# Gated input with tokens on partitions turned by VectorE, queries and keys turned by VectorE, attention's loads at the ordinary rank

## The chip, the core and the metric

The kernel runs on one NeuronCore of a Trainium2 chip. Its engines work at the same time and wait for one another through semaphores: TensorE (PE, matmuls and transposes into the accumulator memory PSUM; its weight loads are listed as PEld), VectorE (DVE), ScalarE (ACT), GpSimd (POOL), and SyncE (SP), which here issues almost all DMAs. Each engine works through its own queue in order. The metric is the time of one execution on the device in microseconds (us); lower is better.

## The reference

One layer of a streaming encoder for 384 tokens: 256 of a prompt and 8 x 16 of running streams, 2048 features, all in float32. The part that the change touches, cut short:

```python
h = rmsnorm(x, norm_mix_g)
proj = h @ w_in        # columns: gated input 2 x 1024 | q 1024 | k 1024 | v 1024 | 8 forget logits | gates 2 x 2048
u = glu_in[..., :D_CONV] * jax.nn.sigmoid(glu_in[..., D_CONV:])
ext = jnp.concatenate([conv_buf, u], axis=1)
z = layernorm(causal_dwconv(ext, conv_dw_w, conv_dw_b), conv_ln_g, conv_ln_b)      # 31 taps
a_out = (z * jax.nn.sigmoid(z)) @ conv_pw_out
new_conv = ext[:, -(CONV_W - 1):]                                                  # an output
q = rmsnorm(q, q_norm_g); k = rmsnorm(k, k_norm_g)                                 # per head of 128; k, v are outputs
logf = jax.nn.log_sigmoid(f_logit + b_forget)
b_out = attn_fn(q, k, v, logf) @ w_att_out     # 8 heads; the 128 cached rows of each stream are read as well
x = x + (gate_a * a_out + gate_b * b_out) @ w_out
...                                            # second norm, up-projection, 3-tap conv, SiLU, down-projection
```

## The kernel before

**Matmuls in three products.** Every large matmul is done on split operands: a float32 is written as hi + lo, and hi x hi, hi x lo and lo x hi are added up in PSUM. A weight tile of 256 rows by up to 512 columns is fetched by SP into `raw` (three buffers, L133 to L139), ScalarE rounds it to `hi` (L145), VectorE makes `lo` as the difference (L146). `plan` lists these tiles in the order in which they are used; `ahead` fetches and splits two or three tiles in advance at a priority 150 places ahead (`SPLIT_AHEAD`), so that the planner which orders the instructions of each engine puts them early. Evacuations of PSUM have 400 (`EVAC_AHEAD`).

**Jobs.** `gemm` (L221) runs jobs one after another. A job of kind "B" has the tokens as stationary operand: for each of 16 k steps, three token blocks of 128 times three products, 512 columns of weights moving (9 matmuls a step). A job of kind "A" has the weights stationary: four blocks of 128 output columns, the 384 tokens moving (12 matmuls of 384 columns a step). The accumulators come from a pool `acc` of 5 PSUM banks and, for the third block of the second job of a pair, from `misc`, of 3 banks, which also serves every transpose and every attention step. After each k step of a job `tick` advances the generators in `sides` by one yield: their PE instructions are written into PE's order at that place. PE's order is the order of the program (`manual_schedule`, L291); the other engines are ordered by the planner. `queued` (L92) ties an instruction behind the last one so tied on its engine. `after(n, fn)` calls fn n ticks later.

**Stages, in PE's order**: 5 warm-up matmuls; the V columns as a pair of jobs with 344 columns each (V0 and V1), while `first_norm` transposes 16 chunks of x on PE (`x_chunk`, L282) and evacuates them as hi and lo of hT (L288, L289), then works out the row factors `rs1` and, by a matmul with a diagonal (L334), the same factors along the free dimension, `rs1b`; V2 alone, with the forget logits; K with `bias_rows` beside it (L483 on; small transposes and matmuls for the forget bias, written to DRAM and read back per head); Q; the gated input (four jobs of kind "A"), with attention and the depthwise conv as sides; the gates (eight jobs), with the rest of the conv and its layer norm; attention's and conv's projections in turns (`AO_PW`); w_out; the up and down projections.

**Attention**, one head every 6 ticks (L651 on): `head_past_keys` turns the cached keys on VectorE (L571) and loads the next head's; `head_operands` transposes the head's queries and keys on PE (L583, L587, three transposes each) and evacuates them (L584, L588); `head_scores` (L595 to L614), `head_probs`, `head_out` and `head_last` follow 4, 9, 11 and 13 ticks after the first. `load_v` fetches the cached values and the bias rows (`bs`) of a head together.

**The conv.** `conv` (L686 on) yields 24 + 7 x 17 + 31 times: channel block c starts at step 24 + 17c. Three ticks before its first tap `fill` builds the padded input `ext`; in it PE transposes the block's last rows (L708, L709), which ScalarE copies (L710, L711) and SP stores (L712, L713). The 31 taps of a block update `ut[:, c]` in place on VectorE (L720, L722); GpSimd adds the finished blocks into `sm` (L725, L727). After the conv's last yield, PE's matmul of `layer_norm` on `sm` (L779) stands in the gates stage. `blocks` (L255) turns token rows into feature rows on VectorE: 16 transposes by 32 x 32 blocks, each on 32 partitions (L259); the later stages use it for mixT, yT, extf and uT.

## Time and profile before

| what | value |
|---|---|
| median of 3 runs (lowest, highest) | 2005.14 us (2003.96, 2006.22) |
| profiled execution | 2005.83 us, span 2003.9 us |
| V columns, 344 wide (first matmul to K) | 7.21 to 85.74 us |
| K and Q | 85.74 to 218.46 us |
| gated input with attention | 218.46 to 390.05 us |
| gates with the rest of the conv | 390.05 to 655.17 us |
| attention's and conv's projections | 655.17 to 786.74 us |
| w_out | 786.74 to 919.73 us |
| up and down projections (last one from 1901.25) | 919.73 us to the end |

The stages are told by the first start of a large matmul of each in the timeline of PE.

How to read it: a row of the timeline is start, duration (both us), engine, line of the program, operation, tiles as out<-in, operands, count, and in brackets the engine's idle time before it with what ended it. A group's row ends in busy time, mean duration in ns, then idle time before and its releasers. Matmuls are pipelined: each lasts longer than the distance to the next one's start.

### The profile page before, as it was taken

Reading aid. Unit: us, or ns where it says so; the run is one execution under the profiler, and the core shown is the slowest. Engines: PE = TensorE matmul, PEld = TensorE weight load, DVE = VectorE, ACT = ScalarE, POOL = GpSimd, SP = SyncE. Lnnn points to the kernel's source line nnn. Section 1 sums busy time; section 2 is a strip of 40 time slices with the busy share of each in tenths; the row PEclk is TensorE's granted clock in tenths of the full one; section 3 lists DMA queues with packets and bytes.
Section 4 is the critical chain, followed back from the end, with each engine's and each line's share of the span. In section 5 each row is a group of like instructions: output and inputs, shape, how many; then the busy total and the mean of one; then the engine's idle time right before and its main releaser. Section 6 shows DMA issues by size and latency. Waiting matters only on the chain.

```text
span 2003.9 us, 24493 instructions
## 1 busy us (share of the span) xinstructions
PE 1992.6 (99%) x9431; PEld 1681.5 (84%) x9431; DVE 1272.2 (63%) x1852; ACT 742.1 (37%) x1077; POOL 87.2 (4%) x216
## 2 busy tenths in 40 slices
PE   8999999999999999999999999999999999999999
PEld 8988999988888887888888888888888888888887
DVE  4435478888765487676867683367673376638663
ACT  5434455433334523334433432233332233323321
POOL 2000001100000000000010000001000000000000
PEclk9999999999999999999999999999999999999999
DMA  6566566444444334534444444444443444344443
GB/s 179 176 175 175 137 163 167 120 140 131 132 134 125 127 121 142 185 121 133 127 137 116 137 127 137 126 127 126 129 135 127 133 120 137 126 129 125 137 157 106
DMA packets 209254, 275.99 MB, mean 138 GB/s; under 512 B 55878, under 2 KB 96729, under 8 KB 209129
## 3 DMA queue, kind: packets, MB, share of 16 engines
q1 hardware_dynamic: 208817, 273.85, 46.3%
q8 instruction: 74, 1.21, 0.2%
q0 software_dynamic: 288, 0.57, 0.2%
q14 instruction: 43, 0.35, 0.1%
q10 hardware_dynamic: 32, 0.01, 0.0%
HBM read 266.98 MB, written 7.86 MB: 137 GB/s over the span
## 4 chain that ended last, share of the span: by engine, by line
PE 95%; DVE 4%; issue 1%; DMA 1%; ACT 0%; SPq 0%; ACTq 0%; DVEq 0%
PE acc L244 28%; PE acc L246 28%; PE acc L245 28%; PE acc L239 2%; PE acc L241 2%; PE acc L240 2%; DVE mixT L259 1%; DVE lo L146 1%; DMA raw<-in_w_in_dram 1%; DVE sgA L843 0%; DVE uT L259 0%; DVE sgA L844 0%; PE misc L636 0%; PE misc L603 0%; PE misc L285 0%
## 5 line engine op out<-in xcount | busy, mean ns | idle before, releaser
L146 DVE TENSOR_TENSOR lo<-raw,hi 128x1024 fp32r<-128x1024 f32 (+2 forms) x481 | 579.6, 1205 | 582.7 <-ACT hi L145 579.0
L145 ACT CAST hi<-raw 128x1024 fp32r<-128x1024 f32 (+2 forms) x481 | 496.0, 1032 | 994.2 <-PE acc L246 869.1
L244 PE MATMUL acc<-hi,xg 128*128 128x512 f32 x1056 | 411.8, 390 | 0.0
L246 PE MATMUL acc<-hi,xg 128*128 128x512 f32 x1056 | 410.9, 389 | 0.0
L245 PE MATMUL acc<-lo,xg 128*128 128x512 f32 x1056 | 410.8, 389 | 0.0
L244 PE MATMUL acc<-hi,hT 128*128 128x512 f32 (+1 forms) x704 | 268.5, 381 | 2.4 <-ACT hT L288 2.4
L246 PE MATMUL acc<-hi,hT 128*128 128x512 f32 (+1 forms) x704 | 266.0, 378 | 0.4 <-DVE hT L289 0.4
L245 PE MATMUL acc<-lo,hT 128*128 128x512 f32 (+1 forms) x704 | 265.8, 377 | 0.0
L244 PEld LDWEIGHTS acc<-hi,xg 128*128 128x128 f32 x1056 | 198.2, 188 | 42.3
L246 PEld LDWEIGHTS acc<-hi,xg 128*128 128x128 f32 x1056 | 198.2, 188 | 41.3
L245 PEld LDWEIGHTS acc<-lo,xg 128*128 128x128 f32 x1056 | 198.2, 188 | 40.6
L244 PE MATMUL acc<-hi,act 128*128 128x512 f32 x528 | 205.5, 389 | 0.5 <-DVE y L1018 0.5
L246 PE MATMUL acc<-hi,act 128*128 128x512 f32 x528 | 205.4, 389 | 0.0
L245 PE MATMUL acc<-lo,act 128*128 128x512 f32 x528 | 205.4, 389 | 0.0
L722 DVE SCALAR_TENSOR_TENSOR ut<-ext,cw,ut 128x384 f32<-128x384 f32 x240 | 151.5, 631 | 6.1
L244 PEld LDWEIGHTS acc<-hi,hT 128*128 128x128 f32 x704 | 132.7, 189 | 25.3 <-ACT hT L288 2.7
L246 PEld LDWEIGHTS acc<-hi,hT 128*128 128x128 f32 x704 | 132.7, 189 | 23.3 <-DVE hT L289 0.7
L245 PEld LDWEIGHTS acc<-lo,hT 128*128 128x128 f32 x704 | 132.8, 189 | 22.2
L259 DVE STREAM_TRANSPOSE extf<-tok 32x384 f32<-32x384 f32 x176 | 100.3, 570 | 30.9 <-ACT tok L954 28.2
L259 DVE STREAM_TRANSPOSE uT<-tok 32x384 f32<-32x384 f32 x176 | 100.3, 570 | 29.7 <-ACT tok L954 26.9
L244 PEld LDWEIGHTS acc<-hi,act 128*128 128x128 f32 x528 | 99.1, 188 | 21.6 <-DVE y L1018 0.9
L245 PEld LDWEIGHTS acc<-lo,act 128*128 128x128 f32 x528 | 99.1, 188 | 20.5
(289 smaller groups left out, 2079.7 us busy)
## 6 DMA issues: line engine op xcount, KB each, us to landing
raw<-in_w_up_dram SPq DMA_DIRECT2D x176, 512.0 KB
raw<-in_w_in_dram SPq DMA_DIRECT2D x96, 512.0 KB
raw<-in_w_down_dram SPq DMA_DIRECT2D x88, 512.0 KB
raw<-in_w_in_dram SPq DMA_DIRECT2D x64, 256.0 KB
raw<-in_w_out_dram SPq DMA_DIRECT2D x32, 512.0 KB
raw<-in_w_att_out_dram SPq DMA_DIRECT2D x16, 512.0 KB
raw<-in_conv_pw_out_dram SPq DMA_DIRECT2D x16, 512.0 KB
raw<-in_w_in_dram SPq DMA_DIRECT2D x23, 344.0 KB
```

The source lines that it names most:

```text
L145: nc.scalar.copy(hi[:, k, :o], raw[:, k, :o])
L146: tt(lo[:, k, :o], raw[:, k, :o], f(hi[:, k, :o]), op=ALU.subtract)
L239: mm(o, hi[:, kk, s], ah, start=st, stop=False)
L240: mm(o, hi[:, kk, s], al, start=False, stop=False)
L241: mm(o, lo[:, kk, s], ah, start=False, stop=sp)
L244: mm(o, ah[:, s], hi[:, kk, :n], start=st, stop=False)
L245: mm(o, ah[:, s], lo[:, kk, :n], start=False, stop=False)
L246: mm(o, al[:, s], hi[:, kk, :n], start=False, stop=sp)
L259: nc.vector.transpose(put(a, slice(32 * b, 32 * b + 32)), src[32 * a:32 * a + 32, b])
L722: stt(o, v, wc, o, op0=ALU.mult, op1=ALU.add)
```

## The change

- **Gated input**: its four jobs have the tokens stationary, as all others. Its result `ur` has tokens on partitions, is multiplied by `rs1` as a per-partition factor, and `blocks` turns it into `ut`. `rs1b` and the matmuls that made it go. `ur` is also the conv state that is stored, by two DMAs after the fourth job; the transposes, copies and 16 DMAs in `fill` go.
- **Queries and keys**: the stages run V0 with V2, then Q, K, and V1 alone. After each, VectorE turns the normed rows by `blocks`: queries into `attT` (whose head's place is later overwritten by the head's output), keys into the memory of `qt`. The transposes on PE and their evacuations in `head_operands` go.
- **Order of attention**: `head_past_keys` becomes part of `head_operands` at tick 1; outputs and last step come at 12 and 14. The steps have a priority 250 places ahead; the loads of the cache and bias rows stay outside it, with values and bias loaded apart (`load_b`).
- **Conv**: CONV_FIRST 32 and CONV_LAG 15 in place of 24 and 17.
- **Accumulators**: `wide=True` puts the third block of every job into `misc`, in all stages but V, V1 and the gated input.
- **Start**: the identity, the splits of the first 20 tiles, the chunks' evacuations, the last squares, the root and the small loads on GpSimd are tied in program order with `queued`; the last squares and the norm come without yields after the last chunk.

```diff
-CONV_FIRST, CONV_LAG = 24, 17
+CONV_FIRST, CONV_LAG = 32, 15
-SPLIT_AHEAD, EVAC_AHEAD = 150, 400
+SPLIT_AHEAD, ATT_AHEAD, EVAC_AHEAD = 150, 250, 400
...
-        nc.scalar.activation(s, m, AF.Sqrt)
+        queued(nc.scalar.activation(s, m, AF.Sqrt), in_first())
...
-        nc.scalar.copy(hi[:, k, :o], raw[:, k, :o])
-        tt(lo[:, k, :o], raw[:, k, :o], f(hi[:, k, :o]), op=ALU.subtract)
+        first = in_first()
+        queued(nc.scalar.copy(hi[:, k, :o], raw[:, k, :o]), first)
+        queued(tt(lo[:, k, :o], raw[:, k, :o], f(hi[:, k, :o]), op=ALU.subtract), first)
...
-    planned(w_in, 0, V_COLS[0], 16, V_COLS[1])
-    for cols in V_COLS[2:] + K_COLS + Q_COLS + GLU_COLS + GA_COLS + GB_COLS:
+    planned(w_in, 0, V_COLS[0], 16, V_COLS[2])
+    for cols in Q_COLS + K_COLS + V_COLS[1:2] + GLU_COLS + GA_COLS + GB_COLS:
...
+    def in_first():
+        return len(plan) >= v_last - 4
...
-    def gemm(jobs, sides=()):
+    def gemm(jobs, sides=(), wide=False):
...
-                nb = 4 if j["kind"] == "A" else NTT
-                j["ps"] = [(misc_tile if j is not js[0] and i == 2 else acc_tile)() for i in range(nb)]
+                j["ps"] = [(misc_tile if i == 2 and (wide or j is not js[0]) else acc_tile)() for i in range(NTT)]
...
+                    if "post" in j:
+                        j["post"]()
...
-        nc.scalar.activation(hi, ps[:, :NT], AF.Identity, scale=g)
-        stt(lo, ps[:, :NT], g, f(hi), op0=ALU.mult, op1=ALU.subtract)
+        with tc.high_priority(offset=EVAC_AHEAD):
+            queued(nc.scalar.activation(hi, ps[:, :NT], AF.Identity, scale=g))
+            queued(stt(lo, ps[:, :NT], g, f(hi), op0=ALU.mult, op1=ALU.subtract))
...
-    gemm([job("B", 16, ha, tok_evac(kt, 512 * i, 512, 0)) for i in range(2)], [bias_rows()])
+    gemm([tok_job(qt, 512 * i, 512, 1) for i in range(2)], [norm_steps, bias_rows()], wide=True)
...
+    def q_panel(n):
+        blocks(qt[:, :, 512 * n:512 * (n + 1)], by_feature(attT[:, 4 * n:4 * n + 4]))
+        for h in range(4 * n, 4 * n + 4):
+            nc.scalar.activation(attT[:, h], attT[:, h], AF.Identity, scale=qgs[:])
+
+    kT = qt[:].rearrange("p t n -> p (t n)").rearrange("p (h x) -> p h x", h=H)
+
+    def k_panel(n):
+        blocks(kt[:, :, 512 * n:512 * (n + 1)], by_feature(kT[:, 4 * n:4 * n + 4]))
+
+    for n in range(2):
+        after(2 + 10 * n, lambda n=n: q_panel(n))
+    gemm([tok_job(kt, 512 * i, 512, 0) for i in range(2)], wide=True)
...
+    for n in range(2):
+        after(3 + 10 * n, lambda n=n: k_panel(n))
+    gemm([v_jobs[1]])
...
     def head_operands(d):
-        hs = d["hs"]
-        d["vc"], d["bs"] = vbs[d["h"]]
-        qT = p_att.tile([P, NT], F32, tag="qT", bufs=2, name="qT")
-        kT = p_att.tile([P, NT], F32, tag="kT", bufs=2, name="kT")
-        ps = misc_tile()
-        for t in range(NTT):
-            tr(ps[:, t * P:(t + 1) * P], qt[:, t, hs], ident[:])
-        nc.scalar.activation(qT[:], ps[:, :NT], AF.Identity, scale=qgs[:])
-        ps = misc_tile()
-        for t in range(NTT):
-            tr(ps[:, t * P:(t + 1) * P], kt[:, t, hs], ident[:])
-        nc.vector.tensor_copy(kT[:], ps[:, :NT])
-        nc.vector.tensor_copy(qz[d["h"] % 2][:, :, :, 0:16], by_stream(qT[:, 2 * P:]))
+        head_past_keys(d)
+        d["bs"] = bss[d["h"]]
+        nc.vector.tensor_copy(qz[d["h"] % 2][:, :, :, 0:16], by_stream(attT[:, d["h"], 2 * P:]))
...
-            for off, step in ((0, head_past_keys), (2, head_operands), (4, head_scores), (9, head_probs),
-                              (11, head_out), (13, head_last)):
+            for off, step in ((1, head_operands), (4, head_scores), (9, head_probs),
+                              (12, head_out), (14, head_last)):
...
-                step(d)
-                if step is head_out and d["h"] + 2 < H:
-                    load_v(d["h"] + 2)
+                with tc.high_priority(offset=ATT_AHEAD):
+                    step(d)
+                if step is head_operands and d["h"] + 1 < H:
+                    load_k(d["h"] + 1)
+                if step is head_probs and d["h"] + 2 < H:
+                    load_b(d["h"] + 2)
+                if step is head_probs and 0 < d["h"] < H - 1:
+                    load_v(d["h"] + 1)
...
     def glu_evac(g):
-        def ev(m, ps):
-            if m < 2:
-                sgb[m] = p_att.tile([P, NT], F32, tag="sgb", bufs=2, name="sgb")
-                tt(sgb[m][:], ps[:, :NT], rs1b[:], op=ALU.mult)
-                nc.scalar.activation(sgb[m][:], sgb[m][:], AF.Sigmoid)
-            else:
-                u = ut[:, 2 * g + m - 2, :]
-                tt(u, ps[:, :NT], rs1b[:], op=ALU.mult)
-                nc.gpsimd.tensor_tensor(u, u, sgb[m - 2][:], op=ALU.mult)
+        def ev(t, ps):
+            sgb = p_att.tile([P, 256], F32, tag="sgb", bufs=2, name="sgb")
+            nc.scalar.activation(sgb[:], ps[:, 0:256], AF.Sigmoid, scale=rs1[:, t:t + 1])
+            stt(ur[:, t, 256 * g:256 * (g + 1)], ps[:, 256:512], rs1[:, t:t + 1], sgb[:], op0=ALU.mult, op1=ALU.mult)
         return ev
+
+    def glu_done(g):
+        def done():
+            blocks(ur[:, :, 256 * g:256 * (g + 1)], by_feature(ut[:, 2 * g:2 * g + 2]))
+            if g == 3:
+                nc.sync.dma_start(sample_conv[0, :, 14:30, :], ur[:, 2, :])
+                nc.sync.dma_start(prompt_conv[0, 0], ur[98:128, 1, :])
+        return done
...
-            ps = misc_tile()
-            tr(ps[:, :P], ut[:, c, 2 * P:], ident[:])
-            tr(ps[:32, P:2 * P], ut[:, c, 224:256], ident[:])
-            nc.scalar.copy(su[:, 0, :], ps[:, :P])
-            nc.scalar.copy(su[:32, 1, :], ps[:32, P:2 * P])
-            nc.sync.dma_start(sample_conv[0, :, 14:30, c * P:(c + 1) * P], su[:, 0, :])
-            nc.sync.dma_start(prompt_conv[0, 0, :, c * P:(c + 1) * P], su[2:32, 1, :])
...
-    gemm([job("A", 16, ha, glu_evac(g)) for g in range(4)], [att_steps, conv_steps])
+    gemm([job(16, ha, glu_evac(g), done=glu_done(g)) for g in range(4)], [att_steps, conv_steps])
```

147 lines of the change are left out of this document (75 added, 72 removed).

## The prediction, made before the changed kernel was built or run

> **What bounds the kernel now.** First the page: the busy times and the chain of work that ended last.
>
> ```profile
> span 2003.9 us, 24493 instructions
> PE 1992.6 (99%) x9431; PEld 1681.5 (84%) x9431; DVE 1272.2 (63%) x1852; ACT 742.1 (37%) x1077; POOL 87.2 (4%) x216
> PE 95%; DVE 4%; issue 1%; DMA 1%; ACT 0%; SPq 0%; ACTq 0%; DVEq 0%
> ```
>
> TensorE is busy for 1992.6 of 2003.9 us and is 95% of the chain. It runs in the order the program writes, so an instruction taken from it shortens the end by its spacing to the next one, unless something else then comes late. A "busy" matmul overlaps its neighbours, so I price by distances between starts in the timeline of TensorE, never by durations.
>
> The profiled execution took 2005.83 us (span 2003.9 and 1.9 around it), 0.7 above the median of 2005.14. The sum below is a difference made on the profiled execution; I subtract it from the median.
>
> **The change part by part.** *Queries and keys, and the shape of the gated input.* The timeline of TensorE in the gated input, around one head's operands:
>
> ```profile
> 235.13 0.49 PE L583 MATMUL misc<-ident,qt 128*128 128x128 f32 x3
> 235.45 0.49 PE L587 MATMUL misc<-ident,kt 128*128 128x128 f32 x3
> 235.96 0.33 PE L240 MATMUL acc<-hT,hi 128*128 128x384 f32 x1
> ...
> 237.37 0.33 PE L239 MATMUL acc<-hT,hi 128*128 128x384 f32 x1
> ...
> 239.80 0.34 PE L241 MATMUL acc<-hT,lo 128*128 128x384 f32 x1
> ```
>
> From 237.37 to 239.80 are 14 steps: 0.1736 us for each 384-column matmul. From the first transpose of a head (235.13) to the second large matmul after it (235.96) pass 0.83 us; one matmul of 0.1736 lies in that, so the six transposes and the slow re-entry cost 0.656. Eight heads: **-5.25 us**.
>
> *The transposes of ut for the conv state, and rs1b.* One tile's row, then two places of the timeline:
>
> ```profile
> L708 PE MATMUL misc<-ident,ut x8: 270/270/330, 274.1 to 548.3; 128*128 128x128 f32 x8
> 548.32 0.27 PE L708 MATMUL misc<-ident,ut 128*128 128x128 f32 x1
> ...
> 548.77 0.40 PE L245 MATMUL acc<-lo,hT 128*128 128x512 f32 x1
> ...
> 79.23 0.32 PE L246 MATMUL acc<-hi,hT 128*128 128x344 f32 x1
> 79.39 0.83 PE L334 MATMUL misc<-r1d,ones 128*128 128x128 f32 x6
> ...
> 80.22 0.32 PE L245 MATMUL acc<-lo,hT 128*128 128x344 f32 x1
> ...
> 718.64 0.39 PE L245 MATMUL acc<-lo,aHL 128*128 128x512 f32 x1
> ...
> 721.59 0.39 PE L246 MATMUL acc<-hi,zt 128*128 128x512 f32 x1
> ```
>
> 718.64 to 721.59 are 13 steps, 0.2269 us for 512 columns. The ut pair costs 548.77 - 548.32 - 0.227 = 0.22, eight times: **-1.8**. rs1b costs 80.22 - 79.39 = 0.83, less one 344-column step of 0.16: **-0.67**.
>
> The gated input's 768 matmuls of 384 columns (4 jobs x 16 x 4 blocks x 3 products) become 576 of 512: 768 x 0.1736 = 133.3 against 576 x 0.2269 = 130.7, **-2.6**. [...]
>
> *The third accumulator in the other pool ("wide").* These are TensorE's waits at job boundaries, timeline again; 721.59 above precedes the first:
>
> ```profile
> 722.16 0.50 PE L244 MATMUL acc<-hi,zt 128*128 128x512 f32 x1 [0.18 <-DVE sgB L828]
> 722.50 0.40 PE L245 MATMUL acc<-lo,zt 128*128 128x512 f32 x1
> ...
> 755.32 0.50 PE L244 MATMUL acc<-hi,zt 128*128 128x512 f32 x1 [0.19 <-DVE sgB L828]
> ...
> 788.45 0.50 PE L244 MATMUL acc<-hi,mix 128*128 128x512 f32 x1 [0.19 <-DVE sgA L843]
> ...
> 1722.67 0.50 PE L244 MATMUL acc<-hi,act 128*128 128x512 f32 x1 [0.48 <-DVE y L1018]
> ```
>
> Each is the third accumulator of a job, waiting for VectorE to empty the first of the job before. With two of five acc tiles per job that reuse comes a job later. The first costs 0.57 - 0.227 + (0.34 - 0.227) = 0.456; two more wait alike, the fourth 0.30 longer: **-2.1**. What is late next is the same evacuation, now with 16 us to spare.
>
> *The start.* Timelines of TensorE, ScalarE and VectorE:
>
> ```profile
> 13.30 0.49 PE L285 MATMUL misc<-ident,xs 128*128 128x128 f32 x3
> 16.23 0.43 PE L244 MATMUL acc<-hi,hT 128*128 128x344 f32 x1 [2.44 <-ACT hT L288]
> ...
> 17.19 0.45 PE L246 MATMUL acc<-hi,hT 128*128 128x344 f32 x1 [0.38 <-DVE hT L289]
> ...
> 20.31 0.49 PE L245 MATMUL acc<-lo,hT 128*128 128x344 f32 x1
> ...
> 12.85 0.77 ACT L145 CAST hi<-raw 128x688 fp32r<-128x688 f32 x1 [3.96 <-DMA raw<-in_w_in_dram]
> 14.94 0.77 ACT L145 CAST hi<-raw 128x688 fp32r<-128x688 f32 x1 [1.32 <-DMA raw<-in_w_in_dram]
> 15.61 0.57 ACT L288 ACTIVATE hT<-misc,gm 128x384 fp32r<-128x384 f32 x1
> 16.53 0.61 DVE L289 SCALAR_TENSOR_TENSOR hT<-misc,gm,hT 128x384 fp32r<-128x384 f32 x1
> ```
>
> TensorE has transposed chunk 2 before 13.30, but ScalarE evacuates it at 15.61, behind two weight splits, the second of which waits for its DMA until 14.94. Queued in program order, chunks 2 and 3 stand between these splits: hi after 12.85 + 0.77, done near 14.2, its lo near 15.1, where now it ends at 17.14. Today's loss: 2.68 us (13.30 to 16.23 less three transposes), 0.64 (two matmuls in 0.96) and 1.36 (11 steps to 20.31 in 3.12 in place of 1.76): 4.7. Left would be about 1.25, if the shorter stop does not bring the slow steps after it; 2.6 if it does. So the gain is 3.45 or 2.1, and nothing if the order on ScalarE stays. I take **-2.8**, between the two. [...]
>
> The other chained waits: ScalarE now has the last squares and the root ahead of the first Q split, with V's evacuations behind them. V's last two k tiles, some 5 us of matmuls, cover it; what sticks out is at most about a split (0.77 above): 0 to 1, **+0.3**.
>
> *What is added for TensorE to wait on.* bias_rows takes three misc tiles at once where now a third is held by the running job, so its last matmul waits for a copy of 0.37 (row below) behind at most one split: 0 to 1.5, **+0.5**. In the gated input an accumulator is now freed by a table load, a sigmoid and a VectorE product, with 12 matmuls (2.7 us) until the next job writes it:
>
> ```profile
> 105.61 0.37 ACT L497 ACTIVATE crow<-misc 8x256 f32<-8x256 f32 x1 [2.00 <-PE misc L496]
> 253.96 1.28 ACT L675 ACT_TABLE_LOAD   x1
> 255.25 0.94 ACT L675 ACTIVATE sgb<-sgb 128x384 f32<-128x384 f32 x2
> ```
>
> 1.28, half of 0.94 and 0.5 for the product, and up to 1 behind a split, make 2.3 to 3.3; attention's matmuls fill two of the three boundaries: 0 to 2, **+0.6**.
>
> *VectorE's new work.* Windows (us of TensorE, its loads, VectorE, ScalarE, GpSimd), groups, and the tile sm:
>
> ```profile
> 153.00:218.50 65.50, 65.50 (x291) 54.24 (x290) 29.20 (x31) 27.88 (x73) 0.00 (x0) 1.00 0.59 165
> 218.50:390.00 171.50, 171.50 (x1239) 165.10 (x1238) 133.73 (x294) 84.69 (x176) 16.04 (x23) 1.00 0.60 149
> 390.00:575.00 185.00, 185.00 (x822) 152.79 (x821) 159.34 (x226) 67.62 (x93) 9.15 (x16) 1.00 0.47 135
> L259 DVE STREAM_TRANSPOSE uT<-tok 32x384 f32<-32x384 f32 x176 | 100.3, 570 | 29.7 <-ACT tok L954 26.9
> L720 DVE TENSOR_SCALAR ut<-ext,cw,col 128x384 f32<-128x384 f32 x8 | 3.8, 478 | 6.1 <-PE misc L709 6.1
> L727 POOL TENSOR_TENSOR sm<-sm,ut x6: 1017/1018/1857, 407.5 to 575.1; 128x384 f32<-128x384 f32 x6
> 617.97 0.81 PE L779 MATMUL misc<-sm,avg 128*128 128x384 f32 x2
> ```
>
> Queries: 32 transposes x 0.57 = 18 us in a 65 us stage where VectorE is busy for 29; keys: 18 more over the 344-column V job moved behind K and the start of the gated input. Both at **nothing**, hidden by large matmuls, with some 20 us until head 0's scores. Gated input: 64 transposes of 192 elements, not in the trace; between half of 0.57 and 0.57, so 18 to 36 us, I take 27, near the middle. Gone are sixteen products and eight copies out of PSUM, about 13. VectorE thus carries 23 to 41 us more between 218 and the layer norm's matmul (617.97). That matmul comes earlier: 174 steps of the conv become 168 (six of 9 x 0.227, 12.3 us), and 12 us were saved ahead of it, so about 594. The last conv sum was added at 576 and the conv has been held to TensorE's order (L720 waits for the ut transposes, each channel at its tick). Freed of it, it fills idle time: 293 us of work in 356 now, 316 to 334 in 376 then. At the 86% of the row from 390 to 575 the lower end takes 367 us and fits, the upper takes 389 and does not. I take **nothing**: an engine that finishes 42 us early (576 against 618) idles because it has run ahead, not because it can do no more; the upper end is a rival.
>
> ScalarE's key and query scaling moves from PSUM evacuations to plain passes; it is at half load. The SP queue issues the same loads for a head in smaller bundles; sixteen state stores become two.
>
> The sum: -5.25 - 1.8 - 0.67 - 2.6 - 2.1 - 2.8 + 0.3 + 0.5 + 0.6 = **-13.8 us**; 2005.14 - 13.8 = **1991.3**.
>
> **The rivals.** *The start stays as it is*: the chain leaves ScalarE's order, or the DMAs set the pace once TensorE is earlier. For it: both splits ahead of 15.61 waited for DMAs; against it, chunk 2 stood ready on TensorE. 2.8 less: 1994.1.
>
> *The conv is late*: TensorE stands at the layer norm's matmul. 334 us of VectorE work at 86% end 389 us after 218, 13 us behind 594; VectorE runs at its full rate while TensorE stands, so about half of that is paid: 7 us, 1998. It decides from 323 us of work (376 x 0.86). For it: windows at 78 and 86% now; against it the 43 us between 575 and 618.
>
> *Weights starve in the gated input (slower than before).* One row of the waits:
>
> ```profile
> ACT hi L145 <- DMA raw<-in_w_in_dram: 13.8, 6, 4.8
> ```
>
> Splits already waited up to 4.8 us for weights behind a head's loads on SP. If cache loads, moved ahead by a shorter stage, or VectorE's transposes ahead of a split eat the three-tile ring at each head, TensorE stops. It decides from 13.8 / 8 = 1.7 us a head; at 2.5 us, 20 us in all, 2011. Against it: TensorE never waited there.
>
> **How the numbers follow.** Forecast 0.63, start 0.15, conv 0.10, starvation 0.08, and 0.04 for stalls that leave it near the old time. The range: start 0.65 better, the 1.25 left of its stop gone and the added waits at nothing (1.4) give 1988; the conv late by 10 us, between its half and its full price, gives 2001. A measurement tells 0.2% (4 us) from no change; faster is below 2001.1: 0.63 + 0.15 + 0.10 = 0.88, same 0.04, slower 0.08.
>
> **What would show it.** No transposes of qt, kt or ut and no r1d on TensorE; 576 matmuls at 0.227 in the gated input, its stage (171.6 us now) near 163; the first stop ended near 15; no waits on sgB, sgA or y at third accumulators; idle TensorE under 1 us at each boundary of the gated input; sm ready ahead of its matmul near 594. The forecast is wrong if TensorE waits for lo, kT or sm.

## The result, and the profile after

The changed kernel takes 2016.2 us (median of 6 runs, 2015.85 to 2019.33) against 2005.23 us of the kernel before (6 runs on the same chip, 2003.96 to 2006.22): the ratio is 1.0059, 95% interval 1.0049 to 1.0069. It is slower by 11 us where 13.8 us less were forecast. The profiled execution took 2019.33 us, 3.1 above the median; the spans of the five other runs lie at 2014.1 to 2014.9 us, its own at 2016.6.

From the page of the changed kernel: the span, the busy times, two rows of the 40 slices, and the chain of work that ended last.

```profile
span 2016.6 us, 24014 instructions
PE 1985.4 (98%) x9169; PEld 1647.9 (82%) x9169; DVE 1315.8 (65%) x1965; ACT 743.3 (37%) x1065; POOL 81.2 (4%) x208
...
PE   9999995999999999999999999999999999999999
PEclk9999997999999999999999999999999999999999
...
PE 87%; DVE 10%; issue 1%; DMA 1%; SPq 0%; ACT 0%; DVEq 0%; ACTq 0%
```

The busy time of TensorE fell by 7 us, as the removed transposes should have it, and the span rose all the same; VectorE's part of the chain grew from 4 to 10%. One slice, the seventh, is half empty (a slice is 50.4 us, so it lies at 302 to 353 us, in the gated input), and the clock that was granted falls in it.

TensorE's three longest waits in the whole kernel (what was waited for; total, times, longest, in us):

```profile
PE misc L646 <- DVE mx L623: 22.1, 1, 22.1
PE misc L310 <- POOL ident L109: 1.5, 1, 1.5
PE misc L617 <- DVE kTs L598: 0.7, 1, 0.7
```

One wait carries it all. TensorE stands at L646, the first matmul of a head's output (`head_out`), which writes a `misc` bank; what it waits for is VectorE's score reduction (L623). The timeline of TensorE around it (start, duration):

```profile
315.26 0.38 PE L609 MATMUL misc<-qt,attT 128*128 128x128 f32 x2
...
316.99 0.64 PE L617 MATMUL misc<-kTs,qz 128*32 128x128 f32 x16 [0.68 <-DVE kTs L598]
...
321.55 0.39 PE L245 MATMUL acc<-hi,hT 128*128 128x512 f32 x1
344.07 0.79 PE L646 MATMUL misc<-vt,pT 128*128 128x128 f32 x2 [22.14 <-DVE mx L623]
```

Head 5's scores are done by 317.6 and hold all three `misc` banks until the reductions have read them. Head 4's output, next on TensorE, needs one of the three. VectorE in that time:

```profile
323.09 1.36 DVE L149 TENSOR_TENSOR lo<-raw,hi 128x1024 fp32r<-128x1024 f32 x1 [1.54 <-ACT hi L148]
324.38 15.16 DVE L737 SCALAR_TENSOR_TENSOR ut<-ext,cw,ut 128x384 f32<-128x384 f32 x22
339.45 1.24 DVE L598 STREAM_TRANSPOSE kTs<-kc 128x1024 f32<-128x1024 f32 x1
340.62 3.19 DVE L737 SCALAR_TENSOR_TENSOR ut<-ext,cw,ut 128x384 f32<-128x384 f32 x5
343.73 0.28 DVE L623 CUSTOM_DVE_ANT_0 pr<-misc,bs 128x128 f32<-128x128 f32 x1
```

It isn't idle and it isn't held up: it works off 27 filter taps of the conv, which nobody needs yet, ahead of the reduction that everybody waits for. In this trace VectorE passed none of the instructions that the planner had put in front: 18 us of taps (15.16 and 3.19) and a turning of cached keys (1.24) ran ahead of a reduction whose operands were ready at 324.8, as the next rows show.

When were the reduction's operands ready? The scores at 317.6, and the bias rows `bs` here (SP issues the first of four loads; GpSimd adds the mask):

```profile
316.18 0.36 SPq L584 DMA_DIRECT2D bs<-c_dr  x1
```

```profile
322.64 0.73 POOL L590 TENSOR_TENSOR bs<-bs,mk 128x256 f32<-128x256 f32 x1 [13.65 <-DMA bs<-c_dr]
323.33 1.43 POOL L591 TENSOR_TENSOR bs<-bs,mk 128x128 f32<-128x128 f32 x1
```

So two things are late: the bias rows by some 7 us (324.8 against 317.6; in the kernel before they were ready 7 us ahead of their scores, 319.5 against 326.2), and, on top of that, the reduction by 19 us more. How many taps stand ahead of it is counted from VectorE's groups in two windows, from 214 us to head 4's first reduction at 299.9 and to head 5's at 343.7:

```profile
L737 DVE SCALAR_TENSOR_TENSOR ut<-ext,cw,ut 128x384 f32<-128x384 f32 x29 | 18.8, 647 | 0.6
...
L737 DVE SCALAR_TENSOR_TENSOR ut<-ext,cw,ut 128x384 f32<-128x384 f32 x60 | 38.7, 645 | 1.6
```

With one first tap (L735) in the one window and two in the other: 30 and 62. Between the reductions of two heads whose scores begin 16.4 us apart on TensorE stand 32 taps of 0.645 us, 20.6 us of work. Counted in the same way (to 308.2 and 325.1 us, with one and two first taps), the kernel before has 28 and 35 there:

```profile
L722 DVE SCALAR_TENSOR_TENSOR ut<-ext,cw,ut 128x384 f32<-128x384 f32 x27 | 17.2, 639 | 0.6
...
L722 DVE SCALAR_TENSOR_TENSOR ut<-ext,cw,ut 128x384 f32<-128x384 f32 x33 | 20.9, 635 | 0.7
```

By head 7's first reduction both kernels have done 62 taps. That much of the conv's work is the same; its place is not.

The stages, by the first start of a large matmul in each, forecast beside them:

| stage | before | after | difference | forecast |
|---|---|---|---|---|
| start to the gated input | 218.46 | 214.15 | -4.3 | -2.7 |
| gated input with attention | 171.59 | 190.48 | +18.9 | -7.25 |
| gates with the conv | 265.12 | 265.41 | +0.3 | -1.8 |
| projections to the end of the span | 1348.71 | 1346.55 | -2.2 | -2.1 |

The whole loss lies in the second row, 26 us worse than forecast: the stop of 22.3, some 3 us lost behind it (the granted clock is 0.50 up to 350.6, for 6.5 us of work), and small waits.

### The profile page after: what moved, and what is told of

Read it like the earlier page. It is cut to its first block, busy times and chain, and to the rows that moved or that the text cites. A ratio compares the mean times of both kernels' runs of the same rounds, so it can differ in the third digit from the quotient of the medians.

```text
span 2016.6 us, 24014 instructions
## 1 busy us (share of the span) xinstructions
PE 1985.4 (98%) x9169; PEld 1647.9 (82%) x9169; DVE 1315.8 (65%) x1965; ACT 743.3 (37%) x1065; POOL 81.2 (4%) x208
## 4 chain that ended last, share of the span: by engine, by line
PE 87%; DVE 10%; issue 1%; DMA 1%; SPq 0%; ACT 0%; DVEq 0%; ACTq 0%
PE acc L243 20%; PE acc L244 20%; PE acc L245 20%; PE misc L244 9%; PE misc L245 9%; PE misc L243 9%; DVE ut L737 5%; DVE lo L149 3%; DVE ut L260 1%; DMA raw<-in_w_in_dram 1%; DVE mixT L260 0%; DVE kTs L598 0%; DMA kc<-in_cache_k_dram 0%; ACT hi L148 0%; PE misc L286 0%
## 5 line engine op out<-in xcount | busy, mean ns | idle before, releaser
L243 PE MATMUL acc<-hi,xg 128*128 128x512 f32 x704 | 274.9, 390 | 0.0
L245 PE MATMUL acc<-hi,xg 128*128 128x512 f32 x704 | 273.9, 389 | 0.0
L244 PE MATMUL acc<-lo,xg 128*128 128x512 f32 x704 | 273.9, 389 | 0.0
L243 PEld LDWEIGHTS acc<-hi,xg 128*128 128x128 f32 x704 | 132.1, 188 | 28.4
L245 PEld LDWEIGHTS acc<-hi,xg 128*128 128x128 f32 x704 | 132.1, 188 | 27.5
L244 PEld LDWEIGHTS acc<-lo,xg 128*128 128x128 f32 x704 | 132.2, 188 | 27.1
L245 PEld LDWEIGHTS acc<-hi,hT 128*128 128x128 f32 x704 | 132.6, 188 | 23.6 <-DVE hT L291 0.7
L737 DVE SCALAR_TENSOR_TENSOR ut<-ext,cw,ut 128x384 f32<-128x384 f32 x240 | 140.9, 629 | 2.0
L245 PE MATMUL misc<-hi,xg 128*128 128x512 f32 x352 | 137.0, 389 | 0.0
L243 PE MATMUL misc<-hi,xg 128*128 128x512 f32 x352 | 137.0, 389 | 0.0
L244 PE MATMUL misc<-lo,xg 128*128 128x512 f32 x352 | 136.9, 389 | 0.0
L243 PE MATMUL acc<-hi,act 128*128 128x512 f32 x352 | 136.9, 389 | 0.0
L244 PE MATMUL acc<-lo,act 128*128 128x512 f32 x352 | 136.9, 389 | 0.0
L245 PE MATMUL acc<-hi,act 128*128 128x512 f32 x352 | 136.9, 389 | 0.0
```

Source lines behind the costliest of these rows:

```text
L243: mm(o, ah[:, s], hi[:, kk, :n], start=st, stop=False)
L244: mm(o, ah[:, s], lo[:, kk, :n], start=False, stop=False)
L245: mm(o, al[:, s], hi[:, kk, :n], start=False, stop=sp)
L737: stt(o, v, wc, o, op0=ALU.mult, op1=ALU.add)
```

## The experiments

Every run below was timed beside the kernel before on the same chip. "Taps" is, for the first reductions of heads 4, 5, 6 and 7, how many taps stand ahead of them on VectorE in that run's trace; the program's text has 1, 7, 13, 23 there for a conv that starts at step 32. The first ten looked for one cause; in all of them but e3, which checks `wide`, the stop had moved.

| run | what | us | ratio (95%) | taps | TensorE's main waits, us |
|---|---|---|---|---|---|
| before | | 2005.2 | | 28, 35, 51, 62 | none over 2.5 |
| after | the change | 2016.2 | 1.0059 (1.0049 to 1.0069) | 30, 62, 62, 62 | reduction 22.1 |
| e1 | bias rows 250 ahead | 2011.6 | 1.0033 (1.0021 to 1.0045) | 31, 31, 53, 62 | vc 6.5; mx at L617 8.9 |
| e2 | keys 250 ahead | 2031.3 | 1.0130 (1.0115 to 1.0145) | 16, 67, 84, 94 | reduction 34.7 |
| e3 | no `wide` | 2018.8 | 1.0066 (1.0049 to 1.0083) | 30, 62, 62, 62 | reduction 21.7 |
| e4 | conv 24, 15 | 2002.1 | 0.9987 (0.9978 to 0.9997) | 33, 45, 62, 76 | reduction 8.7 |
| e5 | all loads 250 ahead | 2018.1 | 1.0066 (1.0050 to 1.0083) | 27, 31, 44, 54 | hi 14.9; lo 5.1 |
| e6 | loads on GpSimd's queue | 2018.2 | 1.0068 (1.0053 to 1.0083) | 30, 31, 40, 50 | attT 16.9 |
| e7 | conv 24, 17 | 2003.3 | 0.9992 (0.9982 to 1.0001) | 33, 45, 62, 62 | reduction 8.9 |
| e8 | loads 120 ahead | 2014.4 | 1.0052 (1.0037 to 1.0067) | 4, 16, 31, 60 | reduction 11.6; lo 8.3 |
| e9 | loads 120, conv 24, 17 | 2005.4 | 1.0003 (0.9994 to 1.0013) | 33, 45, 62, 62 | reduction 7.2; lo 3.5 |
| e10 | steps 0 ahead | 2014.9 | 1.0052 (1.0037 to 1.0067) | 30, 34, 62, 62 | pr 10.4; pz 6.1 |
| e11 | conv 64, 11 | 1999.5 | 0.9974 (0.9964 to 0.9984) | 0, 0, 0, 0 | kTs 3.8 |
| e12 | conv 64, 11, loads 120 | 1997.7 | 0.9964 (0.9950 to 0.9978) | 0, 0, 0, 0 | hi 3.5 |
| e13 | 12 transposes | 2014.0 | 1.0046 (1.0031 to 1.0061) | 31, 62, 62, 66 | reduction 21.7 |
| e14 | 12 transposes, loads 120 | 2008.8 | 1.0019 (1.0010 to 1.0029) | 2, 19, 31, 60 | reduction 12.0; lo 4.5 |
| e15 | taps behind reductions | 2002.9 | 0.9990 (0.9981 to 0.9999) | 1, 7, 13, 23 | kTs 6.4; mx 2.0 |
| e16 | the same, loads 120 | 2000.7 | 0.9982 (0.9973 to 0.9991) | 1, 7, 13, 23 | lo 8.7 |
| e17 | the same, loads 60 | 1996.9 | 0.9961 (0.9947 to 0.9974) | 1, 7, 13, 23 | kTs 4.2 |
| e18 | e17, transposes spread | 1993.4 | 0.9946 (0.9933 to 0.9958) | 1, 7, 13, 23 | kTs 2.3 |

### e1 and e2: one kind of load moved ahead

```diff
                 if step is head_probs and d["h"] + 2 < H:
-                    load_b(d["h"] + 2)
+                    with tc.high_priority(offset=ATT_AHEAD):
+                        load_b(d["h"] + 2)
```

e2 does the same with `load_k(d["h"] + 1)`.

> The changed kernel with one edit: load_b(h + 2), the bias rows of a head, is issued at the attention steps' priority (250 ahead); loads of cached keys and values stay at the ordinary rank. Theory 1 (head 5's bias rows are fetched too late; its reductions stand behind conv taps on VectorE, its three score tiles hold all three misc banks, and TensorE stands 22.1 us at the next head's output, then runs at half clock for some 3 us): the 22.1 us wait is gone, 1991 us (1989 to 1994). Theory 2 (VectorE is overfilled by a conv freed from TensorE's order): a stall of 10 to 22 us stays, at this head or another, 2005 to 2016 us. Theory 3 (a misc bank held by the running job, from wide accumulators): 2014 to 2018 us.

> The changed kernel with one edit: load_k(h + 1), the cached keys, at the attention steps' priority; bias rows and values stay at the ordinary rank. Theory 1: nothing is mended, 2010 us or above, the wait still on a head's reductions. If late cached keys are the cause instead: 1991 us (1989 to 1996).

e1, 2011.6 us: the stop at L646 is gone and others stand in its place, by TensorE's waits:

```profile
PE misc L650 <- DMA vc<-in_cache_v_dram: 6.5, 1, 6.5
PE misc L617 <- DVE mx L627: 5.8, 2, 3.0
PE misc L617 <- DVE mx L625: 3.1, 1, 3.1
```

Now the cached values, still at the ordinary rank, are late, and the three waits at L617, of some 3 us each, end when VectorE has turned the cached keys (at 347.1 in the longest). 1991 us was expected if the bias rows were the cause. e2, 2031.3 us, is the worst of all: with the keys ahead, the bias rows of heads 2 and 5 are ready only at 278.7 and 339.4, some 13 us behind their scores, and 51 taps stand between the reductions of heads 4 and 5, where TensorE stops for 26.3 us. The other stop, of 8.4 us, is for head 2's reductions and has no tap ahead of it: late bias rows do stop TensorE by themselves, for less. The theory that they alone are the cause falls; a load that is moved makes another late.

### e3: the third accumulator back in its own pool

```diff
-                j["ps"] = [(misc_tile if i == 2 and (wide or j is not js[0]) else acc_tile)() for i in range(NTT)]
+                j["ps"] = [(misc_tile if i == 2 and (j is not js[0]) else acc_tile)() for i in range(NTT)]
```

> The changed kernel with wide=True without effect: a single job's three accumulators all come from acc again, in every stage. Theory 1: the 22.1 us wait stays and the four waits at job boundaries return, 2.1 us, less 0.5 for the bias rows' third misc tile: 2018 us (2017 to 2019). Theory 3: the 22 us wait goes, 1993 us.

2018.8 us, 2.5 more than the changed kernel, with the same stop (21.7). From the first matmul of the projections to the end of the span it takes 1348.29 us, the changed kernel 1346.55: the forecast's term for `wide` stands (1.7 us by this), and `wide` has no part in the stop.

### e4 and e7: the conv's start and lag

```diff
-CONV_FIRST, CONV_LAG = 32, 15
+CONV_FIRST, CONV_LAG = 24, 15
```

e7 has 24, 17, as before the change.

> The changed kernel with CONV_FIRST 24 in place of 32 (the conv's steps eight ticks earlier, CONV_LAG 15 kept). Theory 1: head 5's bias rows depend on the order of SP, which this edit shifts; where they come in time the stall is gone and the time 1991 us (1989 to 1995), else 2010 or above. Theory 2: more taps are ready earlier in the gated input, so VectorE is fuller there: at least 2016 us.

> The changed kernel with the convolution's start and lag as before the change (24 and 17 in place of 32 and 15); the loads stay at the ordinary rank on SP. Theory: the loads are as late as in the changed kernel (bias rows of head 5 issued some 20 us after their place), but VectorE's order has no run of over ten taps ahead of a reduction, so what is left is the real lateness of the loads: one or more waits for misc banks of 3 to 10 us, 1997 to 2005 us. Rival 1 (VectorE overfilled): no change beyond 3 us from the run with 24 and 15 (2002 us), as the number of taps is the same. If lateness costs nothing without the long run of taps: 1991 to 1994 us.

2002.1 and 2003.3 us: 13 to 14 us of the loss come and go with the step at which the first tap stands; the 1 us between the two lags is within the noise. In both the stop has moved to head 6 and is 8.7 and 8.9 us long; there the taps between two reductions are 17 instead of 32, and the bias rows are ready at 336.6, 2 us behind the scores.

### e5, e6, e8, e10: the loads' rank and queue

```diff
                 with tc.high_priority(offset=ATT_AHEAD):
                     step(d)
-                if step is head_operands and d["h"] + 1 < H:
-                    load_k(d["h"] + 1)
+                    if step is head_operands and d["h"] + 1 < H:
+                        load_k(d["h"] + 1)
```

and so for `load_b` and `load_v` (e5). In e6 the loads of `load_k`, `load_v` and `load_b` read `nc.gpsimd.dma_start` in place of `nc.sync.dma_start`; in e8 and e9 they stand in `tc.high_priority(offset=120)`; in e10 `ATT_AHEAD` is 0.

> All three loads of a head (cached keys, cached values, bias rows) are given the rank of the head's steps, 250 ahead, nothing else changed. Theory (the loads at the ordinary rank stand behind weight fetches in SP's order, and VectorE's order was laid out for their late coming): keys and bias rows are ready ahead of their scores for every head, no wait of TensorE for a misc bank over 3 us stands in the gated-input stage, and the time is 1990 to 1995 us. Rival 1 (VectorE is simply overfilled between 290 and 345 us by the 32 columns' filter taps and the block transposes): a stop of 5 us or more for a misc bank stays, 2000 to 2016 us. Rival 2 (the transfers are late for want of DMA bandwidth, wherever they stand): earlier issues push the weights back, TensorE waits for lo by several us, 1998 to 2012 us.

> The three loads stay at the ordinary rank but are issued on GpSimd's queue in place of SP's, so no weight fetch that waits for a raw buffer stands ahead of them. Theory (SP's order holds them up): bias rows land ahead of the scores of every head, the long stop for a misc bank is gone, 1990 to 1997 us. Rival 1 (it is the rank itself, by which VectorE's taps are laid ahead of the reductions whatever queue the loads use): a stop of 5 us or more for a misc bank, 2000 to 2016 us. Rival 2 (DMA bandwidth): the same issue times or later landings, weights late, 1998 to 2012 us.

> All three loads of a head are placed 120 ahead: between the ordinary rank of the changed kernel and the 250 of the run before. Theory (only the place of the loads in SP's queue is wrong: at 0 they come behind fetches that wait for a raw buffer, at 250 the bias rows' wait for their buffer holds the fetches): bias rows of head 5 are issued before 310 us and no fetch waits for them, so neither a wait for a misc bank over 3 us nor one for hi or lo over 1 us, 1990 to 1995 us. Rival 1 (VectorE is overfilled from 290 us on by taps and block transposes, and the reductions are late whatever the loads do): a stop of 5 us or more for a misc bank, 1999 us or more. Rival 2 (DMA bandwidth): waits for hi or lo of several us, 1997 to 2010 us.

> As the run before, with the convolution's start and lag of the kernel before the change (24 and 17). Theory: with the loads in time the place of the taps matters little, as VectorE's order holds no run of eight or more taps ahead of a reduction in either: 1990 to 1995 us, within 2 us of the run before. Rival 1 (VectorE overfilled): better than the run before by more than 3 us where that one has a stop, as taps start earlier; or a stop of 5 us or more in both, 1999 us or more.

> The changed kernel with the steps of a head at the ordinary rank too (0 ahead in place of 250), so steps and loads have one rank, as in the kernel before. If the loads' place in SP's queue is what is late: bias rows of heads 5 and 6 still come 3 us or more after their scores, a wait for a misc bank of 5 to 12 us stays, 1998 to 2006 us. If it is the gap between the two ranks: the steps' VectorE work moves back to where the loads are, TensorE's order being fixed by the program, and the stop goes: 1990 to 1995 us.

Five misses of the theory that the loads' place is the whole of it. In e5 the bias rows of every head were ready ahead of its scores (head 5: 298.6 against 343.1), and it still took 2018.1 us. Its waits and SP's queue show why:

```profile
PE acc L243 <- ACT hi L148: 14.9, 3, 6.4
PE acc L244 <- DVE lo L149: 5.1, 5, 3.1
```

```profile
301.05 1.19 SPq L139 DMA_DIRECT2D raw<-in_w_in_dram  x2
309.27 0.34 SPq L584 DMA_DIRECT2D bs<-c_dr  x1
...
311.38 0.92 SPq L139 DMA_DIRECT2D raw<-in_w_in_dram  x2
```

No weights are issued between 302.2 and 311.4. The bias rows have two buffers, and this load, head 6's, has to wait until head 4's reductions, from 307.1 on, have freed one; the weights' fetches are behind it on the same queue. This is the forecast's rival of starved weights, called up by loads that stand too early.

In e6 the bias rows were in time too (308.8; the scores were done at 318.2), and the stop at head 4's output is gone. A new one of 16.9 us came from GpSimd: its queue issued the four loads of a head's keys 4 us apart, and the conv's fill, which has to clear two strips on GpSimd (L725, L726), stood behind them, so that VectorE, at a first tap, waited 18.2 us for it and everything behind that tap with it:

```profile
PE misc L609 <- DVE attT L663: 16.9, 1, 16.9
```

So e6 says nothing against SP's order, and nothing for it. e8 says most: bias rows of heads 5, 6 and 7 ready 12 us or more ahead of their scores, 29 taps between the reductions of heads 6 and 7, and TensorE standing 11.6 us at the same L646 two heads later. e10 shows that it isn't the gap between the ranks of steps and loads either. What the stops for a reduction share, but for the 8.4 us in e2, is a run of 17 to 51 taps ahead of it.

### e11 to e14: the taps out of the stage, or the transposes

e11 has `CONV_FIRST, CONV_LAG = 64, 11`, e12 the loads 120 ahead as well. With 11 steps between columns the one tile of cached conv rows (`sc`) is loaded with the next column's before a column has used its own, so that the conv there works on another column's cached rows. In e13 and e14 (loads 120 ahead) three transposes a group do what sixteen did; the move of a 32x32 block to its own group of partitions is left out, so the conv's input stands in the wrong places:

```diff
-            blocks(ur[:, :, 256 * g:256 * (g + 1)], by_feature(ut[:, 2 * g:2 * g + 2]))
+            flat = ut[:, 2 * g:2 * g + 2].rearrange("p c x -> p (c x)")
+            for t in range(NTT):
+                nc.vector.transpose(flat[:, 256 * t:256 * (t + 1)], ur[:, t, 256 * g:256 * (g + 1)])
```

> The changed kernel with the convolution's first tap at its 64th step, which is past the gated-input stage, and 11 steps from column to column in place of 15, so that the last column ends 4 steps later than in the changed kernel. The loads stay at the ordinary rank. Theory A (VectorE is full in the gated-input stage, since the 64 block transposes stand there beside taps, and what is late on it stops TensorE): no taps in the stage, so no stop for a misc bank above 2 us there, 1990 to 1996 us. Theory B (the loads' place in SP's queue is a cause of its own): bias rows of heads 5 and 6 still 5 to 10 us behind their scores, one or two stops of 5 to 10 us, 1999 to 2008 us. A late convolution would show as a wait for sm, or in the LayerNorm, behind 500 us.

> The same convolution with the loads 120 ahead. Theory A: as the run before within 2 us, 1990 to 1996 us. Theory B: better than the run before by its stops, 1990 to 1996 us too, with that run at 1999 or more. Neither (both loads and taps out of the way and a stop left): above 1999 us.

> The changed kernel with the gated input turned by three block transposes of 128x256 per group in place of sixteen of 32x192: the turning inside each 32x32 block stays, the move of a block to another group of 32 partitions is left out, so the convolution's input is in the wrong places. Takes some 18 us of VectorE's work out of the stage. Theory A (the transposes are what overfills VectorE): the stop of 22 us shrinks below 8 us, 1990 to 2002 us. Theory B (the loads' place): the stop stays at 10 us or more, 2003 to 2017 us.

> The same twelve transposes with the loads 120 ahead. If both are needed for the stop to go: no wait for a misc bank or for lo above 2 us, 1990 to 1995 us, against 2014.4 us with the 64 transposes. If the transposes' time on VectorE is not a cause: stops of 10 us or more as with the 64, 2008 to 2015 us.

With no tap in the stage no wait for a reduction is left, at either rank of the loads: 1999.5 and 1997.7 us, both faster than the kernel before, though above the 1990 to 1996 expected if VectorE's taps were the whole. What is left is 3.8 us for turned keys in e11, and 3.5 us for a `hi` and 1.2 us for `lo` in e12.

With the transposes cut to twelve the stops stay: 21.7 us in e13, 12.0 in e14, in spite of 19 us less work for VectorE (4.6 us of transposes in place of 23.6) and idle time on it ahead of the stop (10.6 us busy in the 16 from 284 to 300 us in e14). So it isn't that VectorE has too much to do. What is left is the order of its work, which the next two runs change.

### e15 and e16: the order alone

One dependency without a semaphore keeps a tap behind the last reduction that stands before it in the program; nothing else in the program changes. e16 has the loads 120 ahead too.

```diff
+            red = nc.vector.tensor_tensor_reduce(out=v, in0=sp_[:, :n * P], ...
...
+        reduced[0] = red.ins.name
...
+            tc.add_manual_dep(d.ins, reduced[0], mybir.DependencyInfo(
+                mybir.DependencyClass.NoSync, mybir.DependencyReason.DATA), reason="taps")
```

> The changed kernel with one rule for VectorE's order: no filter tap goes ahead of the score reductions that stand before it in the program (7 taps ahead of head 5's reductions, as in the program, in place of the 62 that the trace of the changed kernel has there). The loads stay at the ordinary rank. Theory C (the stop is the run of taps that was laid ahead of the reductions; the late loads are the lesser part): the stop of 22 us goes, what is left is the bias rows' own lateness, 3 to 9 us at heads 5 to 7, 1994 to 2004 us. Theory B (the loads' place in SP's queue is the whole): as the changed kernel within 5 us, 2011 us or more. If the taps are then late for the LayerNorm: waits behind 500 us.

> The same rule with the loads 120 ahead, where bias rows came in time but a run of 29 taps stood ahead of head 7's reductions. Theory C: no wait for a misc bank, lo or hi above 2 us in the gated-input stage, 1990 to 1995 us, which is below both kernels and is the forecast's own time. Theory A (VectorE is overfilled whatever its order): a stop of 5 us or more stays, 1999 us or more.

e15, 2002.9 us: 13.3 us less than the changed kernel with the same work on every engine and the bias rows of head 5 hardly earlier (322.3 against 315.9 for the scores). TensorE's waits:

```profile
PE misc L619 <- DVE kTs L598: 6.4, 2, 3.8
PE misc L649 <- DVE mx L625: 2.0, 1, 2.0
```

Only the 2.0 us is a load's own lateness, that of the bias rows of head 5 (22.1 us in the changed kernel at the same place). The 6.4 us for the keys of heads 6 and 7 are VectorE's order again. SP issued the last of these loads at 324.3 and 340.7, and they were in by 328.3 and 344.8 us; VectorE turned the keys at 337.2, behind a split that waited for its `hi`, and at 357.4:

```profile
355.22 1.15 DVE L740 SCALAR_TENSOR_TENSOR ut<-ext,cw,ut 128x384 f32<-128x384 f32 x2
356.29 1.22 DVE L149 TENSOR_TENSOR lo<-raw,hi 128x1024 fp32r<-128x1024 f32 x1
357.42 1.24 DVE L598 STREAM_TRANSPOSE kTs<-kc 128x1024 f32<-128x1024 f32 x1
```

e16 has neither wait and gets one of 8.7 us for lo, the larger part at 345 us. VectorE there:

```profile
342.93 3.03 DVE L260 STREAM_TRANSPOSE ut<-ur 32x192 f32<-32x192 f32 x8
345.98 0.29 DVE L666 COPY attT<-misc 128x128 f32<-128x128 f32 x1
346.28 3.06 DVE L260 STREAM_TRANSPOSE ut<-ur 32x192 f32<-32x192 f32 x8
349.38 1.25 DVE L598 STREAM_TRANSPOSE kTs<-kc 128x1024 f32<-128x1024 f32 x1
350.55 1.18 DVE L149 TENSOR_TENSOR lo<-raw,hi 128x1024 fp32r<-128x1024 f32 x1
```

The split that TensorE waits for stands behind the sixteen block transposes of a group, 6.1 us, and those of the cached keys. Its `hi` was ready at 343.3. So 2000.7 us missed the 1990 to 1995 that were expected, and by its number fits the rival of an overfilled VectorE; e17 and e18, with the same work in 1996.9 and 1993.4 us, speak against that rival.

### e17 and e18: between, and the transposes spread

e17 is e15 with the loads 60 ahead. e18 is e17 with this, and each transpose behind the last split but one on VectorE:

```diff
-            blocks(ur[:, :, 256 * g:256 * (g + 1)], by_feature(ut[:, 2 * g:2 * g + 2]))
+            rows, put = ur[:, :, 256 * g:256 * (g + 1)], by_feature(ut[:, 2 * g:2 * g + 2])
+            if g < 3:
+                for b in range(4):
+                    after(1 + 2 * b, lambda b=b: one_block(rows, put, b))
+            else:
+                blocks(rows, put)
```

> The rule for the taps with the loads 60 ahead, between the two runs before (0: waits for kTs of 6.4 us and 2.0 us for a bias row; 120: waits for lo of 8.7 us, of which 6.0 us in one where the splits stand behind a group's block transposes on VectorE). If both remaining stops are set by where the loads stand: bias rows and keys in time, splits no longer behind the loads' work, waits for misc banks and lo together 2 to 5 us, 1992 to 1997 us. If the splits' wait comes from the block transposes alone: a wait for lo of 4 us or more stays, 1997 to 2001 us.

> As the run before, with the sixteen block transposes of the first three groups handed out four at a time, two steps of the contraction apart, each behind the last but one split on VectorE in place of all together at the group's end. If the transposes of 6 us at a group's end are what the splits wait behind (the forecast put them at nothing): 1 to 4 us less than the run before, 1990 to 1994 us, no wait above 2 us in the stage. If they cost nothing: within 1 us of the run before.

1996.9 and 1993.4 us: 6.0 us for the loads' place, once the taps are out of the way, and 3.5 us for spreading the transposes. In e17 TensorE waits for no split. Its one long wait, 4.2 us, is for the turned keys of head 7, which were in by 334.7 us and are turned at 352.1, behind transposes and eight taps (the rule keeps taps behind reductions only):

```profile
345.08 2.68 DVE L260 STREAM_TRANSPOSE ut<-ur 32x192 f32<-32x192 f32 x7
...
348.91 3.26 DVE L741 SCALAR_TENSOR_TENSOR ut<-ext,cw,ut 128x384 f32<-128x384 f32 x6
352.09 1.24 DVE L598 STREAM_TRANSPOSE kTs<-kc 128x1024 f32<-128x1024 f32 x1
```

In e18 they are turned at 348.6, the wait is 2.3 us, and TensorE has half its clock for 3.4 us behind it in place of 6.7 (0.79 granted on average from 350 to 366 us in e17). The edit moves the transposes and the planner laid the taps anew with them, so how much of the 3.5 us belongs to which was not separated. e18 is faster than the kernel before by 0.54% (0.42 to 0.67%). Its longest wait is

```profile
PE misc L623 <- DVE kTs L602: 2.3, 1, 2.3
```

Its gated input takes 167.77 us; without the 2.4 us by which head 7's scores end later there than head 6's do, and the 1.6 us of slow matmuls behind them (eight spacings of 0.42 us, as the changed kernel has at a granted 0.50 from 347.69, in place of 0.23), it would be 163.8, where the forecast had put the stage near 163.

## Why the prediction was wrong

The forecast of 1991.3 us was the time of a kernel whose VectorE never keeps TensorE waiting. That kernel can nearly be had, 1993.4 us, but the change as it stands isn't it. The 24.9 us between, by the medians:

| from | to | us | what |
|---|---|---|---|
| after 2016.2 | e15 2002.9 | 13.3 | taps ahead of the reductions |
| e15 2002.9 | e17 1996.9 | 6.0 | the loads' rank |
| e17 1996.9 | e18 1993.4 | 3.5 | block transposes at a group's end, and taps, ahead of head 7's keys |
| e18 1993.4 | forecast 1991.3 | 2.1 | left; e18 has one stop, for kTs |

The steps in this order of removal; in another order each takes another share (loads first, e8, gives 1.8). The kernel before took 2004.4 to 2005.2 us beside these runs, so the smaller steps are good to about 1 us.

**The step that failed** is in "VectorE's new work": "Freed of it, it fills idle time", and the "nothing" that was drawn from it. The step compared sums: us of VectorE work in a stage against the us that the stage lasts. They did fit: with the same work in another order (e15) the stop is gone, and the conv was never late. But the taps that had waited for TensorE's ut transposes, "each channel at its tick", now wait only for a group's products, and the planner laid 32 of them between two reductions, where before it had 7. That the freed dependency is what let it do so is argued; no run put it back. It isn't the whole of it: with the dependency gone and the conv at 24, 17 as before (e7), 12 taps stand there, at most 17 between any two heads, and the time is 2003.3 us. The later start of the conv, which the forecast counted only as six steps less, makes the run of 32 as well. An engine that takes its work in order can stop another without being full: VectorE was busy for 159 of the stage's 190.48 us in the changed kernel, and TensorE waited 22.1 us for it. The forecast priced the work and not the order.

**The loads at the ordinary rank** got half a sentence, "the same loads for a head in smaller bundles", at no cost. The steps that use them went 250 places ahead, the weights' fetches were at 150, the loads at 0; the bias rows of head 5 reached SP at 316.2, when their scores had begun. Measured: 6.0 us with the taps in order. Only a part of it is a load that comes late (in e15 the bias rows of head 5, 2.0 us of waiting and 3.4 us at half the clock behind it, by the 0.90 granted on average from 316 to 333 us); the keys were in early, and what moved for them is the order on VectorE. No term of the sum stood for it, and none of the rivals either.

**The 64 block transposes.** Their size was right: 0.369 us each, 23.6 us in all, inside the 18 to 36 and near the 27 taken, by their group in the changed kernel:

```profile
L260 DVE STREAM_TRANSPOSE ut<-ur 32x192 f32<-32x192 f32 x64 | 23.6, 369 | 1.1
```

"At nothing" was wrong, again by order: sixteen stand together at a group's end. Ahead of a split they are most of a wait of 6.0 us (e16); spreading them gave 3.5 us (e17 to e18), with the taps that moved beside them.

**What held.** Queries and keys turned on VectorE cost TensorE no wait, and with the ut products and the shape of the gated input they make the 163.8 us worked out above for e18 (171.6 - 5.25 - 2.6 + 0.6 = 164.3 by the terms). The waits of that stage's accumulators (0.4 us on ur) and of the bias rows' matmul (0.2 us) are under their terms of 0.6 and 0.5. `wide` gives 2.2 us by the last row of the stages and 1.7 by e3 (2.1 forecast). The conv was in time for the layer norm: no wait for sm. The start, in TensorE's timeline:

```profile
13.38 0.49 PE L286 MATMUL misc<-ident,xs 128*128 128x128 f32 x3
14.50 0.42 PE L243 MATMUL acc<-hi,hT 128*128 128x344 f32 x1 [0.62 <-ACT hT L290]
...
15.71 0.32 PE L243 MATMUL acc<-hi,hT 128*128 128x344 f32 x1
```

The stop ends at 14.50 (near 15 was said). 1.12 less 0.24 for the transposes, and 1.21 for three matmuls in place of 0.47, leave 1.6 of the 4.7 us: a gain of 3.1, inside 2.1 to 3.45, and the granted clock does not fall there (1.00 in every us from 12 to 22). Large matmuls also begin 1.2 us earlier (6.04, 7.21 before), which the forecast didn't have. The transposes of ut for the conv state were to give 1.8 us in the gates; e4 and e13 show 1.5 there (263.66 against 265.12), e18 0.9 (264.26), with five matmuls between 519 and 541 us begun 0.5 us late in all. Where the rest went was not tried.

**The rivals.** The start did change, and the conv was not late. The rival on the slow side, starved weights, had the sign and came within 6 us (2011), but by luck, for a reason that isn't in the changed kernel's trace: TensorE waits 0.5 us for lo there and not at all for weights. The sentence on what would prove the forecast wrong named lo, kT and sm; the wait that came was for a bank.

**What stays open.** Why the planner lays a run of taps where it does was not shown. It moves with the rank of the loads and the start of the conv (head 5 in the changed kernel, 6 in e1 and e4, 7 in e8), as it would if the planner takes the reductions to be late there and fills the gap; that is argued, not shown. The waits for lo in e8, and 2.7 of the 8.7 us in e16, were not taken apart: how much of them is the loads' work on SP and how much the order on VectorE.

## What to carry to other kernels

Where an engine works in order, ask of each stage not only whether its work fits but what stands in front of the instruction that others wait for; deferrable work that is freed of a dependency should get a new one, as cheap as "not ahead of that reduction" (13 us here). When the users of some data are moved ahead, their loads have to be placed anew, and not at the far end: behind the fetches they come late, ahead of them a load that waits for its own buffer stops the fetches (for 9.2 us in e5; 0, 60 and 250 places: 2002.9 and 1996.9 us with the taps in order, 2018.1 us without). If a stop moves from head to head as one cause after another is removed, look for what the stops share.

## What the runs showed of the hardware

At these three stops the granted clock fell late, twice when the stop was already over. In the changed kernel TensorE stands from 321.8 to 344.07 us; the clock granted in windows (the column after the five engines' times) falls from 1.00 to 0.50 at 326.7, 5 us into the stop, and is back at 350.6, 6.5 us after work began again. In e18 TensorE stands for 2.3 of the 3 us up to 350, and the clock holds through 1.3 us of work behind that, to 351.3:

```profile
347.00:350.00 3.00, 0.67 (x8) 0.44 (x10) 2.92 (x9) 0.00 (x0) 0.00 (x0) 1.00 1.03 306
350.00:351.00 1.00, 1.00 (x18) 0.76 (x19) 0.74 (x6) 0.48 (x2) 0.00 (x0) 1.00 0.27 66
351.00:352.00 1.00, 1.00 (x5) 0.81 (x4) 1.00 (x6) 0.62 (x3) 0.00 (x0) 0.66 0.00 0
```

So a stop that put the scores off by 2.4 us cost 4.0. In the kernel before TensorE stands for 2.44 us until 16.23 and for 0.38 until 17.19, and the clock falls to 0.50 at 17.45, when work has begun again, and is back at 20.9. What sets the moment of the fall was not shown.

Loads of the same shape were issued by GpSimd's queue some 4 us apart (311.18, 315.87, 320.19 and 323.94 us in e6) where SP issued four in 5.9 us (e16).
